# GLA in whole token groups, with new charges for two engines in the recorder of a hybrid decoder kernel

## Chip, cores and metric

The kernel runs on one core of one Trainium2 chip. The metric is device time in microseconds (us), the median of several runs. TensorE multiplies matrices; VectorE, ScalarE and GpSimd (DVE, ACT and POOL in the profile) do the rest; SyncE (SP) issues the DMAs.

## What is computed

A two-layer decoder trunk runs over 1072 tokens: 16 meta tokens and 8 sample sequences of 4 tokens (together 48 leading tokens) and a prompt of 1024. In each layer one input projection feeds four mixers with four heads each; their outputs are joined, projected, normalised, and followed by a SwiGLU feed-forward and a second normalisation.

```
for l in range(DEPTH):                      # 2
    proj = x @ w_in[l]                      # 1024 -> 3864
    o_a = gated DeltaNet(...)               # 4 heads, 64x64 state
    o_b = HGRN2(...)                        # 4 heads, 64x64 state
    o_c = GLA(c_q, c_k, c_v, log_sigmoid(c_lr @ gla_wg + gla_bg) / 16)   # 4 heads, 32x64 state
    o_d = RetNet(...)                       # 4 heads, 64x64 state
    x = layer_norm(ALPHA * x + concat(o_a, o_b, o_c, o_d) @ w_out[l])
    x = layer_norm(ALPHA * x + (silu(x @ w_g[l]) * (x @ w_u[l])) @ w_d[l])
```

HGRN2 and GLA share one recurrence: with b the running sum of the log gates, a chunk's scores are q_t k_s exp(b_t - b_s) for s <= t, its output is scores times v plus (q exp(b)) times the carried state, and the state goes on with exp(b_last).

## The kernel before

Tokens lie in three groups of 304, 384 and 384 columns (`GROUPS`). The first group holds the 48 leading tokens and two chunks of 128; the others hold three chunks each. Features lie on the 128 partitions.

**Main stream.** The dense products (`main`: `layer_in`, `layer_out`, `layer_ffn`) run through each weight tile for the three groups. Each product is three matmuls of split operands (high and low halves in float32r), all with the full 128x128 array, recorded by `mm` at L839. Weights come in by DMA and are split by ScalarE (L861) and VectorE (L870).

**Mixers.** They run while `layer_in` still projects for later mixers. Four workers, each with an arena of 3072 columns (`Arena`), take jobs (a mixer or half of its heads, and a token group) from a queue in the order delta, GLA, HGRN2, retention. `task_units` cuts a job into units: the leading tokens, then the whole chunks. `UNITS` takes all chunks of a group as one unit (two in the first group, three in the others); `HALVES` cuts the second and third group into a unit of two chunks and one of one chunk, and is used for GLA alone. A layer so has 24 units of the other mixers (six jobs with four units each) and six of GLA.

**One unit of GLA or HGRN2** (`gated`). A 128x128 score block is built in steps. The steps of `upper` (64, 32) fill the off-diagonal parts, those of `low` (for GLA s8, s2, s1; for HGRN2 s8 and b8) the 32x32 blocks on the diagonal. Each step subtracts gate sums, takes exponentials on ScalarE, multiplies by q and k, runs small products with tiles of 32 rows, and copies or selects the result out of PSUM. Then come k and v transposed (`rows`, L845 for the transposes), the state (`states_and_out`), the output, and the head norm (`norm_out`; `head_mean` there makes two matmuls with full tiles). GLA packs four heads of 32 features into 128 partitions, the others two heads of 64.

**Order.** Nothing is written in the order it runs. Each thread (main stream, workers, weights, norms) yields operations, and the recorder (`run`, `emit`) plays them on a clock of its own and each time appends the operation that could start first to its engine's program. An operation's charge (for example 68 + 1.042 n ns for VectorE with n columns) and `LATENCY` (from its end until another engine may use the result) make that clock; `SHARED` is added where VectorE and GpSimd work on SBUF side by side. A pair such as `copy2` or `tt2` goes to the engine that would end first. The engines then run their programs in order and wait on semaphores. Small tiles and full tiles don't mix on TensorE: `run` holds a change of tile mode back for a while (`HOLD`, `SLACK`), and `emit` charges `DRAIN` for it.

Of the kernel before, what the change touches and what calls it, by code (L numbers as in the profile page):

```python
# [334 lines left out]

LATENCY = {"PE": 196.0, "DVE": 138.0, "ACT": 158.0, "POOL": 92.0}
SHARED = 300.0

# [97 lines left out]
class Kern:  # L436
# [437 lines left out]
    def stt(self, out, a, s, b, op0, op1):  # L874
# [3 lines left out]
        if isinstance(s, V):  # L878
            rd.append(s)
            sc = s.ap  # L880
            ptr = 61
        return Op("DVE", 68 + ptr + 1.042 * out.n,
                  lambda: self.nc.vector.scalar_tensor_tensor(out=out.x(), in0=a.x(), scalar=sc, in1=b.x(), op0=op0, op1=op1),  # L883
# [8 lines left out]
    def ts(self, out, a, s1, op0, s2=None, op1=None, eng="DVE"):  # L892
# [14 lines left out]
        if eng == "DVE":  # L907
            return Op("DVE", 68 + ptr + rate * out.n, lambda: self.nc.vector.tensor_scalar(out=out.x(), in0=a.x(), **kw), rd, (out,))  # L908
        return Op("POOL", 245 + 0.83 * out.n, lambda: self.nc.gpsimd.tensor_scalar(out=out.x(), in0=a.x(), **kw), rd, (out,))

    def dcopy(self, out, a):
        rate = 1.042 if a.sp == "p" else 0.52
        return Op("DVE", 68 + rate * out.n, lambda: self.nc.vector.tensor_copy(out=out.x(), in_=a.x()), (a,), (out,))  # L913

# [3 lines left out]
    def pred(self, out, mask, data):  # L918
        return Op("DVE", 68 + 1.042 * out.n,
                  lambda: self.nc.vector.copy_predicated(out=out.x(), mask=mask, data=data.x()), (data, out), (out,))  # L920

    def scan(self, out, d0, d1):
        return Op("DVE", 68 + 1.042 * out.n,
                  lambda: self.nc.vector.tensor_tensor_scan(out=out.x(), data0=d0.x(), data1=d1.x(), initial=0.0, op0=MUL, op1=ADD),
                  (d0, d1), (out,))

    def t32(self, out, a):
        return Op("DVE", 68 + 1.042 * out.n, lambda: self.nc.vector.transpose(out=out.x(), in_=a.x()), (a,), (out,))

# [5 lines left out]
    def recip(self, out, a):  # L935
        return Op("DVE", 68 + 8.4 * out.n, lambda: self.nc.vector.reciprocal(out=out.x(), in_=a.x()), (a,), (out,))

    def red(self, out, a):
        return Op("DVE", 68 + 1.042 * a.n,
                  lambda: self.nc.vector.tensor_reduce(out=out.x(), in_=a.x(), axis=mybir.AxisListType.X, op=ADD), (a,), (out,))  # L940
# [72 lines left out]
    def ln_sums(self, srcs, m, st):  # L1013

        nc = self.nc
        for k, s in enumerate(srcs):
            o = st.ap[0:m, 6 * k:6 * k + 6]
            yield Op("DVE", 68 + 1.05 * 512, lambda o=o, s=s: nc.vector.bn_stats(out=o, in_=s.x()), (s,), (st,))  # L1018
        o, x = st.ap[0:m, 12:14], st.ap[0:m, 0:12]
# [517 lines left out]
    def gated(self, A, l, u, q, k, vs, b, es, K, first, low, upper, S, S0, bo_out, names, sf, spent):  # L1537
# [17 lines left out]
        a4 = None if lead else at.r("p (h a t) -> p h a t", h=H, t=128)  # L1555
        for m in list(first) if lead else list(upper) + list(low):
            wk = wq = None
# [27 lines left out]
            for j in range(H // 2):  # L1585
# [28 lines left out]
                if m == 64:  # L1614
                    yield self.copy2(a4[0:64, hs, :, 64:128], bp[0:64, :, 0:64 * nb].r("p h (a t) -> p h a t", a=nb))
                elif m == 32:
                    for z in range(2):
                        r = slice(64 * z, 64 * z + 32)
                        yield self.copy2(a4[r, hs, :, 64 * z + 32:64 * z + 64],
                                         bp[r, :, 0:32 * nb].r("p h (a t) -> p h a t", a=nb))  # L1620
# [22 lines left out]
        qe = A.alloc(n)  # L1643
        yield self.tt2(qe, q, eb, MUL)
        ke = A.alloc(n)
# [7 lines left out]
        yield self.act(AF.Exp, ke, ke, scale=es)  # L1653
        yield self.tt2(ke, ke, k, MUL)
        kt = A.alloc(nb * 128)
        A.free(b)
# [5 lines left out]
        self.free(*spent)  # L1662
        yield from self.states_and_out(A, l, u, qe, kt, vts, at, S, S0, eb, None, K, H, bo_out, names, sf)

# [64 lines left out]

    def states_and_out(self, A, l, u, qe, kt, vts, at, S, S0, eb, gam, K, H, bo_out, names, sf):  # L1730

# [15 lines left out]
        else:  # L1747
# [4 lines left out]
            for a in range(nb):  # L1752
                sc = gam[0] if gam else eb[:, 128 * a + 127:128 * a + 128]
                yield self.stt(S[a + 1], S[a], sc,
# [8 lines left out]
        for j in range(nv):  # L1763
# [10 lines left out]
            for k in range(2):  # L1774
                for a in range(nb):
                    for hh in range(2):
                        h = 2 * j + hh
                        o = bo[64 * hh:64 * hh + 64, bl * a:bl * a + bl]
                        x = h * nb + a
                        if k:  # L1780
                            r = slice(K * h, K * h + K)
                            yield self.mm(o, S[a][r], qe[r, 128 * a:128 * a + 128], False, a == nb - 1)
                        else:
                            yield self.mm(o, vv(h, a), at[:, 128 * x:128 * x + 128], a == 0, False)
            if j == nv - 1:
                A.free(qe, at, *vts)
            yield from bo_out(j, bo)
# [153 lines left out]
    def ret(self, A, l, hh, g, J):  # L1941
# [24 lines left out]
        for x in self.task_units(A, J, g, self.i["sr"][l, hh]):  # L1966
# [42 lines left out]
            if u[0] + n == gn:  # L2009
                self.free(*ins)  # L2010
            yield from self.states_and_out(A, l, u, qe, kt, [vt], at, S, S0, None, gam, 64, 2, done,
                                           (None, "rs%d%d" % (l, hh)), sf)
# [646 lines left out]
```

## Time and profile before

| | |
|---|---|
| median of 3 runs | 3121.15 us (3118.95 to 3122.83) |
| the profiled execution, its own time | 3118.43 us |
| its span, first to last instruction | 3116.3 us |
| busy: TensorE, VectorE, ScalarE, GpSimd | 2987.8, 1750.8, 1111.4, 391.2 us |
| mean granted TensorE clock | 0.986 of full |

The profile cuts the span into slices and gives each engine's busy share, lists groups of equal instructions with their mean duration and the idle time before them, and names for each wait who ended it. The first layer's mixers run from about 100 to 690 us, its feed-forward from about 800 to 1540; the second layer's mixers from 1560 to 2176 us, its feed-forward until about 3070. A matmul's row shows a longer duration than the distance to the next one, since matmuls overlap; distances are read from start times.

### The profile page before, as it was taken

How to read it: one execution, taken by the hardware profiler on the slowest of the kernel's cores; microseconds unless marked ns; L12 is line 12 of the kernel's file. 1: busy time of each engine (PE TensorE's matmuls, PEld its weight loads, DVE VectorE, ACT ScalarE, POOL GpSimd, SP SyncE). 2: the span in 40 equal slices, each digit the busy share in tenths (PEclk: the TensorE clock that was granted, in tenths of full speed). 3: DMA queues.
4: the chain of work that ended last, by engine and by line, in shares of the span. 5: the costliest groups of instructions: out<-in, count | busy, mean ns of one | idle time of the engine just before them, and what ended most of it. 6: DMA issues, size and time to landing. Idle time of an engine off the chain costs nothing.

```text
span 3116.3 us, 65676 instructions
## 1 busy us (share of the span) xinstructions
PE 2987.8 (96%) x27758; PEld 2712.0 (87%) x27758; DVE 1750.8 (56%) x4142; ACT 1111.4 (36%) x2313; POOL 391.2 (13%) x444
## 2 busy tenths in 40 slices
PE   7999999999999999999999999999899999999996
PEld 5788887888999999999977888888689999999996
DVE  8877668577533333333598676684674333333336
ACT  5445667443311111111263456664342111111113
POOL 3411111000600000000033111110014000000000
PEclk9999999999999999999999999999999999999998
DMA  6311121351211111111142111124311111111112
GB/s 208 107 50 34 60 65 53 105 183 37 75 48 41 41 48 49 47 48 41 46 137 86 36 55 62 59 65 139 122 55 55 46 50 48 48 42 47 48 41 76
DMA packets 120741, 210.54 MB, mean 68 GB/s; under 512 B 32304, under 2 KB 81200, under 8 KB 120320
## 3 DMA queue, kind: packets, MB, share of 16 engines
q1 hardware_dynamic: 120448, 206.36, 20.7%
q8 instruction: 217, 3.56, 0.5%
q14 instruction: 76, 0.62, 0.1%
HBM read 162.08 MB, written 39.84 MB: 65 GB/s over the span
## 4 chain that ended last, share of the span: by engine, by line
PE 66%; DVE 7%; ACT 2%; DMA 2%; issue 1%; POOL 1%; SPq 0%; DVEq 0%; ACTq 0%; POOLq 0%
PE banks L839 64%; DVE H L870 2%; PE banks L845 1%; DVE P L870 1%; DVE H L883 1%; DVE R L870 1%; ACT H L864 1%; ACT R L861 1%; DMA H<-OF 0%; DVE H L1018 0%; POOL R L872 0%; DVE H L908 0%; DMA P<-H 0%; ACT P L864 0%; DVE P L913 0%
## 5 line engine op out<-in xcount | busy, mean ns | idle before, releaser
L839 PE MATMUL banks<-R 128*128 128x384 f32 (+3 forms) x11840 | 2091.1, 332 | 28.3 <-DVE H L883 9.4
L839 PEld LDWEIGHTS banks<-R 128*128 128x128 f32 x11840 | 1926.0, 190 | 91.3 <-issue 14.1
L870 DVE TENSOR_TENSOR H<-H,banks 128x512 f32<-128x512 f32 (+5 forms) x708 | 401.1, 570 | 522.3 <-PE banks L839 518.0
L870 DVE TENSOR_TENSOR R<-H,R 128x1024 fp32r<-128x1024 f32 (+5 forms) x376 | 358.9, 967 | 444.7 <-ACT R L861 442.0
L861 ACT CAST R<-H 128x1024 fp32r<-128x1024 f32 (+4 forms) x361 | 285.9, 806 | 817.7 <-PE banks L839 720.8
L839 PE MATMUL banks<-R,P 128*128 128x512 f32 x1584 | 371.7, 394 | 0.0
L839 PEld LDWEIGHTS banks<-R,P 128*128 128x128 f32 x1584 | 296.2, 188 | 66.7 <-issue 0.5
L864 ACT ACTIVATE H<-H 128x384 f32<-128x384 f32 (+12 forms) x477 | 204.5, 445 | 206.2 <-DVE H L1020 86.0
L872 POOL TENSOR_TENSOR H<-H 128x256 f32<-128x256 f32 (+8 forms) x206 | 194.6, 962 | 290.6 <-ACT H L864 116.1
L839 PE MATMUL banks<-H 32*32 32x32 f32 (+11 forms) x5884 | 187.2, 224 | 18.8 <-DVE H L870 6.3
L872 POOL TENSOR_TENSOR P<-H,P 128x384 fp32r<-128x384 f32 (+1 forms) x22 | 39.5, 1798 | 1274.0 <-ACT P L861 1271.7
L839 PEld LDWEIGHTS banks<-H 32*32 32x32 f32 (+6 forms) x5884 | 133.3, 120 | 75.2 <-issue 39.3
L839 PE MATMUL banks<-P 32*32 32x32 f32 (+14 forms) x6240 | 181.1, 214 | 15.7 <-DVE P L870 9.8
L839 PEld LDWEIGHTS banks<-P 32*32 32x32 f32 (+10 forms) x6240 | 132.0, 117 | 63.4 <-issue 27.5
L861 ACT COPY H<-banks 128x384 f32<-128x384 f32 (+14 forms) x313 | 115.8, 376 | 181.2 <-PE banks L839 143.3
L870 DVE TENSOR_TENSOR H<-H 128x384 f32<-128x384 f32 (+14 forms) x389 | 155.3, 417 | 43.8 <-ACT H L864 25.7
L861 ACT CAST P<-H 128x304 fp32r<-128x304 f32 (+2 forms) x132 | 64.3, 487 | 284.5 <-DVE H L870 284.5
L864 ACT ACTIVATE H<-banks 128x384 f32<-128x384 f32 (+4 forms) x166 | 70.7, 430 | 222.5 <-PE banks L839 215.5
L839 PE MATMUL banks<-P,R 128*128 128x304 f32 (+1 forms) x1056 | 147.4, 299 | 0.0
L839 PEld LDWEIGHTS banks<-P,R 128*128 128x128 f32 x1056 | 145.9, 188 | 0.0
L845 PE MATMUL banks<-H 128*128 128x128 f32 (+4 forms) x642 | 109.0, 290 | 30.3 <-DMA H<-in_cst 7.7
L845 PEld LDWEIGHTS banks<-H 128*128 128x128 f32 (+4 forms) x642 | 74.7, 142 | 62.7 <-ACT H L864 17.3
(86 smaller groups left out, 1637.9 us busy)
## 6 DMA issues: line engine op xcount, KB each, us to landing
H<-in_wst SPq DMA_DIRECT2D x208, 512.0 KB, 3.3
XR<-H SPq DMA_DIRECT2D x12, 512.0 KB, 3.4
GF<-H SPq DMA_DIRECT2D x32, 192.0 KB, 1.9
H<-XR SPq DMA_DIRECT2D x4, 1536.0 KB, 7.0
H<-XR SPq DMA_DIRECT2D x42, 128.0 KB, 2.7
XR<-H SPq DMA_DIRECT2D x42, 128.0 KB, 2.0
H<-OF SPq DMA_DIRECT2D x27, 192.0 KB, 4.6
H<-in_xin SPq DMA_DIRECT2D x8, 512.0 KB, 8.2
```

The costliest lines, as they stand in the source:

```text
L839: return Op("PE", cost, lambda: self.nc.tensor.matmul(out=out.x(), lhsT=lhsT.ap, rhs=rhs.ap, start=start, stop=stop), (lhsT, rhs), (out,), ...
L845: return Op("PE", 0.83 * p + 2.5, lambda: self.nc.tensor.transpose(out=out.x(), in_=in_.ap, identity=i.ap), (in_,), (out,), 20, None, tile ...
L861: fn = lambda: self.nc.scalar.copy(out=out.x(), in_=in_.x())
L864: fn = lambda: self.nc.scalar.activation(out=out.x(), in_=in_.x(), func=f, scale=s, bias=b)
L870: lambda: self.nc.vector.tensor_tensor(out=out.x(), in0=a.x(), in1=b.x(), op=op), (a, b), (out,))
L872: lambda: self.nc.gpsimd.tensor_tensor(out=out.x(), in0=a.x(), in1=b.x(), op=op), (a, b), (out,), 27.0)
L883: lambda: self.nc.vector.scalar_tensor_tensor(out=out.x(), in0=a.x(), scalar=sc, in1=b.x(), op0=op0, op1=op1),
```

## The change

GLA takes all chunks of a group as one unit, as the other mixers do. To fit the arena, a unit now makes the low steps first and takes the full score blocks, one buffer for each pair of heads, only ahead of step 64; exp(b) is reused as q exp(b), with only its last columns copied to `eb`; the transposed v overwrites v where there are two v tiles. The charges of VectorE and ScalarE rise by 25 and by 52 to 54 ns an operation, `LATENCY` falls by 18 and 48 ns, `SHARED` rises by 50. `stt`, `ts`, `pred`, `scan`, `t32`, `recip`, `red` and `ln_sums` change like `tt` (68 becomes 93).

```diff
-LATENCY = {"PE": 196.0, "DVE": 138.0, "ACT": 158.0, "POOL": 92.0}
-SHARED = 300.0
+LATENCY = {"PE": 196.0, "DVE": 120.0, "ACT": 110.0, "POOL": 92.0}
+SHARED = 350.0
...
     def act(self, func, out, in_, scale=1.0, bias=0.0):
-        cost = out.n * 0.833 + (51 if in_.sp == "p" else 93)
+        cost = out.n * 0.833 + (105 if in_.sp == "p" else 145)
...
     def tt(self, out, a, b, op, eng="DVE"):
-            return Op("DVE", 68 + 1.042 * out.n,
+            return Op("DVE", 93 + 1.042 * out.n,
...
     def dcopy(self, out, a):
-        rate = 1.042 if a.sp == "p" else 0.52
-        return Op("DVE", 68 + rate * out.n, ...
+        rate = 1.042 if a.sp == "p" or len(out.ap.shape) > 2 else 0.52
+        return Op("DVE", 93 + rate * out.n, ...
...
     def gated(...):
-            at = A.alloc(nb * H * 128)
-            yield self.zero(at)
             ac = A.alloc(nb * H * 32)
             yield self.zero(ac)
-        for m in list(first) if lead else list(upper) + list(low):
+        for m in list(first) if lead else list(low) + list(upper):
+            if not lead and m == upper[0]:
+                at = [A.alloc(nb * 256) for _ in range(H // 2)]
+                for x in at:
+                    yield self.zero(x)
...
             for z in range(4):
-                yield self.dcopy(a4[r, :, :, 32 * z:32 * z + 32], dst[r].r("p h (a t) -> p h a t", t=32))
+                for j, x in enumerate(a4):
+                    yield self.dcopy(x[r, :, :, 32 * z:32 * z + 32],
+                                     dst[r, 2 * j:2 * j + 2].r("p h (a t) -> p h a t", t=32))
...
+            eb, qe = A.alloc(nb), eb
+            yield self.dcopy(eb, qe.r("p (a c) -> p a c", c=128)[:, :, 127])
+            yield self.tt2(qe, q, qe, MUL)
...
-        vts = [A.alloc(nb * 128) for _ in vs]
+        place = not lead and len(vs) > 1
+        vts = vs if place else [A.alloc(nb * 128) for _ in vs]
...
     def task_units(self, A, J, g, state):
-        units = (HALVES if J.key[1] == "c" else UNITS)[g]
+        units = UNITS[g]
```

What the recorder then writes differs on every engine. Counted over the whole programs, before and now: matmuls 21462 and 21446, VectorE instructions 4144 and 3948, ScalarE 2315 and 2174, GpSimd 449 and 462, SyncE 797 and 781. The TensorE program goes from full tiles to smaller ones or back 700 times before and 648 times now, that is, it has 350 and 324 runs of small-tile products.

**TensorE, first layer, the s8, s2 and s1 products of GLA** (rows `32x48`: 32 partitions, 48 columns; R is the region of split operands, so `banks<-R` rows are the main stream; H and P are the regions with the arenas; x counts equal rows). First, the program before at the one-chunk unit of the second token group: each step is a run of 16, and the same happens once more for the third group.

```order
L839 MATMUL banks<-H 32x48 x16
L839 MATMUL banks<-R 128x304 x10
L839 MATMUL banks<-R 128x384 x15
L839 MATMUL banks<-H 32x48 x16
L839 MATMUL banks<-R 128x48 x2
L839 MATMUL banks<-R 128x384 x9
L839 MATMUL banks<-H 32x48 x16
```

Then the changed program, where a step covers three chunks at once.

```order
L839 MATMUL banks<-P_74 32x512 x2
L839 MATMUL banks<-R 128x384 x18
L839 MATMUL banks<-H 32x48 x48
L839 MATMUL banks<-R 128x384 x20
L839 MATMUL banks<-R 128x304 x7
L839 MATMUL banks<-P_74 32x48 x32
L839 MATMUL banks<-R 128x304 x39
L839 MATMUL banks<-H 32x48 x48
```

The three runs of the one-chunk unit are gone, its products stand in the longer runs. The last `32x48` row of GLA in this layer comes after 1560 matmuls of the R region before and after 1125 now.

**TensorE, second layer, the end of the mixers**, where the output projection begins (`128x288` and `128x512` rows of R) and retention's last units are left. The program before:

```order
L839 MATMUL banks<-H 128x128 x6
L839 MATMUL banks<-P_14763 64x512 x2
L845 MATMUL banks<-H 128x128 x2
L839 MATMUL banks<-R 128x288 x15
L845 MATMUL banks<-H 128x128 x2
L839 MATMUL banks<-H 128x128 x4
L845 MATMUL banks<-H 128x128 x3
L839 MATMUL banks<-R 128x288 x4
L845 MATMUL banks<-H 128x128 x3
L839 MATMUL banks<-R 128x288 x5
L839 MATMUL banks<-R 128x512 x3
L839 MATMUL banks<-H 128x128 x6
```

The changed program:

```order
L839 MATMUL banks<-H 128x128 x6
L839 MATMUL banks<-P_14602 64x512 x2
L845 MATMUL banks<-H 128x128 x2
L839 MATMUL banks<-R 128x288 x24
L845 MATMUL banks<-H 128x128 x2
L839 MATMUL banks<-H 128x128 x4
L839 MATMUL banks<-P_14602 64x64 x4
L845 MATMUL banks<-H 128x128 x6
L839 MATMUL banks<-H 64x64 x6
L839 MATMUL banks<-P_14602 64x128 x4
L839 MATMUL banks<-P_14602,H 64x128 x2
L839 MATMUL banks<-P_14602 64x128 x2
```

The 24 products `128x288`, which stood in three pieces between the small ones, and the first `128x512` ones (3, 3 and 1) no longer separate them; the row of small products that begins behind the 24 goes on for 14 rows.

## Rows read from the trace of the kernel before

**Rows 1.** The page: span, and busy us of each engine.

```profile
span 3116.3 us, 65676 instructions
PE 2987.8 (96%) x27758; PEld 2712.0 (87%) x27758; DVE 1750.8 (56%) x4142; ACT 1111.4 (36%) x2313; POOL 391.2 (13%) x444
```

**Rows 2.** Stretches: from:to, length, busy PE, PEld, DVE, ACT, POOL, clock, DMA share, GB/s.

```profile
0.00:100.00 100.00, 77.97 (x515) 61.17 (x516) 89.79 (x251) 58.12 (x132) 35.76 (x47) 0.95 0.55 187
100.00:690.00 590.00, 560.28 (x8332) 484.75 (x8331) 412.05 (x1237) 316.92 (x729) 84.39 (x130) 0.98 0.26 81
690.00:800.00 110.00, 105.06 (x619) 90.39 (x618) 86.16 (x155) 47.34 (x88) 20.46 (x12) 0.98 0.18 55
800.00:1400.00 600.00, 600.00 (x3492) 575.08 (x3491) 217.39 (x315) 103.87 (x162) 47.09 (x33) 1.00 0.15 47
1560.00:2176.00 616.00, 586.48 (x8562) 512.43 (x8561) 447.72 (x1365) 336.48 (x785) 121.47 (x167) 0.98 0.25 77
2176.00:2340.00 164.00, 145.76 (x904) 121.52 (x903) 121.25 (x230) 66.56 (x132) 25.13 (x18) 0.96 0.30 97
2340.00:3000.00 660.00, 660.00 (x3887) 631.94 (x3886) 240.87 (x353) 116.15 (x182) 48.78 (x34) 1.00 0.14 47
3060.00:3117.00 57.00, 32.22 (x179) 28.55 (x177) 45.43 (x91) 19.80 (x33) 1.29 (x1) 0.81 0.21 76
```

**Rows 3.** Waits of TensorE, 100 to 690 us: total us, times, longest.

```profile
PE banks L839 <- DVE P L870: 8.7, 10, 1.4
PE banks L845 <- DVE P L870: 2.5, 3, 1.4
PE banks L839 <- DVE H L870: 2.4, 5, 1.1
```

**Rows 4.** Waits of TensorE, 1560 to 2176 us.

```profile
PE banks L839 <- DVE P L870: 9.9, 11, 3.0
PE banks L839 <- DVE H L870: 4.2, 6, 1.8
```

**Rows 5.** Timeline of TensorE, runs of small products: start, us, what, count.

```profile
89.07 0.31 PE L839 MATMUL banks<-P 32*32 32x32 f32 x8
89.31 1.42 PE L839 MATMUL banks<-R 128*128 128x304 f32 x8
...
215.08 0.62 PE L839 MATMUL banks<-P 32*32 32x32 f32 x48
215.63 1.39 PE L839 MATMUL banks<-R 128*128 128x304 f32 x8
...
226.57 0.91 PE L839 MATMUL banks<-P 32*32 32x32 f32 x80
227.41 0.82 PE L839 MATMUL banks<-R 128*128 128x304 f32 x4
```

**Rows 6.** Groups by shape, VectorE and ScalarE: busy us, mean ns, idle before.

```profile
L870 DVE TENSOR_TENSOR P<-P 128x256 f32<-128x256 f32 x44 | 18.7, 425 | 2.9 <-PE banks L839 2.3
L870 DVE TENSOR_TENSOR H<-H 128x128 f32<-128x128 f32 x58 | 17.3, 303 | 9.3 <-ACT H L864 7.2 <-PE banks L839 1.8
L870 DVE TENSOR_TENSOR P<-P 128x384 f32<-128x384 f32 x29 | 17.1, 588 | 0.3
```

**Rows 7.** Timeline, VectorE and ScalarE, equal instructions back to back.

```profile
3105.90 2.43 DVE L870 TENSOR_TENSOR H<-H 128x512 f32<-128x512 f32 x4
...
1613.44 1.34 ACT L864 ACTIVATE H<-H 128x384 f32<-128x384 f32 x3
```

**Rows 8.** Timeline of TensorE, second layer, end of the mixers; idle before in brackets.

```profile
2183.14 0.39 PE L839 MATMUL banks<-R 128*128 128x32 f32 x1 [4.18 <-ACT R L861]
...
2191.19 0.88 PE L845 MATMUL banks<-H 128*128 128x128 f32 x6 [2.15 <-DVE H L870]
...
2196.14 2.73 PE L839 MATMUL banks<-R 128*128 128x288 f32 x15 [1.84 <-DVE H L883]
```

**Rows 9.** Stretch around those waits (columns as in Rows 2).

```profile
2172.00:2202.00 30.00, 20.56 (x120) 17.64 (x119) 23.34 (x48) 16.99 (x38) 3.50 (x4) 0.83 0.81 269
```

More of the change, by code (lines that the diff above doesn't have):

```diff
@@ L881, in stt @@
             ptr = 61
-        return Op("DVE", 68 + ptr + 1.042 * out.n,
+        return Op("DVE", 93 + ptr + 1.042 * out.n,
                   lambda: self.nc.vector.scalar_tensor_tensor(out=out.x(), in0=a.x(), scalar=sc, in1=b.x(), op0=op0, op1=op1),
@@ L918, in pred @@
     def pred(self, out, mask, data):
-        return Op("DVE", 68 + 1.042 * out.n,
+        return Op("DVE", 93 + 1.042 * out.n,
                   lambda: self.nc.vector.copy_predicated(out=out.x(), mask=mask, data=data.x()), (data, out), (out,))
     def scan(self, out, d0, d1):
-        return Op("DVE", 68 + 1.042 * out.n,
+        return Op("DVE", 93 + 1.042 * out.n,
                   lambda: self.nc.vector.tensor_tensor_scan(out=out.x(), data0=d0.x(), data1=d1.x(), initial=0.0, op0=MUL, op1=ADD),
@@ L927, in t32 @@
     def t32(self, out, a):
-        return Op("DVE", 68 + 1.042 * out.n, lambda: self.nc.vector.transpose(out=out.x(), in_=a.x()), (a,), (out,))
+        return Op("DVE", 93 + 1.042 * out.n, lambda: self.nc.vector.transpose(out=out.x(), in_=a.x()), (a,), (out,))
     def zero(self, out, eng="POOL"):
@@ L935, in recip @@
     def recip(self, out, a):
-        return Op("DVE", 68 + 8.4 * out.n, lambda: self.nc.vector.reciprocal(out=out.x(), in_=a.x()), (a,), (out,))
+        return Op("DVE", 93 + 8.4 * out.n, lambda: self.nc.vector.reciprocal(out=out.x(), in_=a.x()), (a,), (out,))
     def red(self, out, a):
-        return Op("DVE", 68 + 1.042 * a.n,
+        return Op("DVE", 93 + 1.042 * a.n,
                   lambda: self.nc.vector.tensor_reduce(out=out.x(), in_=a.x(), axis=mybir.AxisListType.X, op=ADD), (a,), (out,))
@@ L1017, in ln_sums @@
             o = st.ap[0:m, 6 * k:6 * k + 6]
-            yield Op("DVE", 68 + 1.05 * 512, lambda o=o, s=s: nc.vector.bn_stats(out=o, in_=s.x()), (s,), (st,))
+            yield Op("DVE", 93 + 1.05 * 512, lambda o=o, s=s: nc.vector.bn_stats(out=o, in_=s.x()), (s,), (st,))
         o, x = st.ap[0:m, 12:14], st.ap[0:m, 0:12]
@@ L1554, in gated @@
             dst, mrows = ac.r("p (h x) -> p h x", h=H), 128
-        a4 = None if lead else at.r("p (h a t) -> p h a t", h=H, t=128)
-        for m in list(first) if lead else list(upper) + list(low):
+        for m in list(first) if lead else list(low) + list(upper):
[3 more added lines that the diff above has]
+                    yield self.zero(x)
+                a4 = [x.r("p (h a t) -> p h a t", h=2, t=128) for x in at]
             wk = wq = None
@@ L1642, in gated @@
         yield self.act(AF.Exp, eb, b, scale=es)
-        qe = A.alloc(n)
-        yield self.tt2(qe, q, eb, MUL)
+        if lead:
+            qe = A.alloc(n)
+            yield self.tt2(qe, q, eb, MUL)
+        else:
+            eb, qe = A.alloc(nb), eb
+            yield self.dcopy(eb, qe.r("p (a c) -> p a c", c=128)[:, :, 127])
+            yield self.tt2(qe, q, qe, MUL)
         ke = A.alloc(n)
@@ L1654, in gated @@
         yield self.tt2(ke, ke, k, MUL)
+        A.free(b)
         kt = A.alloc(nb * 128)
-        A.free(b)
         yield from self.rows(ke, nb, bl, [lambda x: iter([self.copy2(kt[0:bl], x[0:bl, 0:nb * 128])])])
         A.free(ke)
-        vts = [A.alloc(nb * 128) for _ in vs]
+        place = not lead and len(vs) > 1
+        vts = vs if place else [A.alloc(nb * 128) for _ in vs]
         for v, vt in zip(vs, vts):
             yield from self.rows(v, nb, bl, [lambda x: iter([self.copy2(vt[0:bl], x[0:bl, 0:nb * 128])])])
-        self.free(*spent)
-        yield from self.states_and_out(A, l, u, qe, kt, vts, at, S, S0, eb, None, K, H, bo_out, names, sf)
+        self.free(*(spent[:-len(vs)] if place else spent))
+        yield from self.states_and_out(A, l, u, qe, kt, vts, at, S, S0, eb, None, K, H, bo_out, names, sf, place, spent)
     def stepped(self, A, name, q, k, b, es, n):
@@ L1752, in states_and_out @@
             for a in range(nb):
-                sc = gam[0] if gam else eb[:, 128 * a + 127:128 * a + 128]
+                sc = gam[0] if gam else eb[:, a:a + 1]
                 yield self.stt(S[a + 1], S[a], sc,
@@ L1783, in states_and_out @@
                         else:
-                            yield self.mm(o, vv(h, a), at[:, 128 * x:128 * x + 128], a == 0, False)
+                            yield self.mm(o, vv(h, a), at[j][:, 128 * x:128 * x + 128], a == 0, False)
+            A.free(at[j])
             if j == nv - 1:
-                A.free(qe, at, *vts)
+                A.free(qe, *(() if place else vts))
+                if place:
+                    self.free(*spent[-len(vts):])
             yield from bo_out(j, bo)
@@ L2010, in ret @@
                 self.free(*ins)
-            yield from self.states_and_out(A, l, u, qe, kt, [vt], at, S, S0, None, gam, 64, 2, done,
+            yield from self.states_and_out(A, l, u, qe, kt, [vt], at if lead else [at], S, S0, None, gam, 64, 2, done,
                                            (None, "rs%d%d" % (l, hh)), sf)
```

12 lines of the change are left out of this document (6 added, 6 removed).

## Prediction

> **What bounds the kernel.** I read the page first. TensorE is busy 2987.8 of 3116.3 us, and no other engine more than 56% of the span [rows 1]. So the time is TensorE's work plus its gaps, 128.5 us, and an engine that is merely relieved gives nothing. Next I read the stretches, to see where the gaps are. In both feed-forwards TensorE is busy for all of 600 and all of 660 us: nothing to gain there, and the change touches nothing there but the order on engines that have time [rows 2]. The gaps lie in five places: 22.0 us in the first 100 us, 29.7 in the first layer's mixers (590 less 560.28), 29.5 in the second layer's (616 less 586.48), and 4.9 and 18.2 us around the output projection and the first norm of each layer [rows 2]; the rest, some 24, is nearly all at the very end, where the last norm has no matmuls left beside it [rows 2]. GLA runs only in the two mixer stretches, so its stake is their 59.2 us. Third, the waits in them: the longest total is VectorE's results in the arenas, 8.7 and 9.9 us in waits of about 0.9 us, followed by other waits on VectorE [rows 3, 4]. These are waits that the recorder did not foresee: it had main-stream matmuls at hand for most of the stretch and would have put some in between, had its clock shown the operand late.
>
> **TensorE's work.** 16 matmuls go, the head norm's two for each of the eight GLA outputs that were cut in two; the columns stay the same, so I take 0. Everything else TensorE computes is the same products in another order. What shrinks is the number of runs of small tiles: 350 to 324. The price of a run that doesn't depend on its length comes from start times: from the first small product to the next main one a run of 48 takes 0.55 us (215.08 to 215.63) and one of 80 takes 0.84 (226.57 to 227.41), so a product adds 0.29 / 32 = 0.009 us and 0.12 us is left; a run of 8 takes 0.24 (89.07 to 89.31), which leaves 0.17 [rows 5]. 26 runs at 0.15 are **-3.9 us**; the bounds are 0, if the saved runs only grow elsewhere, and -6.5, at 0.25 with a gap ahead of the run too.
>
> **VectorE and ScalarE.** A merged VectorE operation takes 588 ns instead of 425 + 303, so 140 ns less [rows 6]. 196 instructions fewer are about 27 us of its 1750.8, and 141 on ScalarE are of the same size. By themselves these give 0: TensorE covers them, being busy 95% of both stretches [rows 2]. The cover is gone only where TensorE already waits, which is the next term. Added inside a unit are four more copies of diagonal blocks (two buffers instead of one) and a copy of the last columns of exp(b). They stand in a chain of some 40 operations while other workers' products and the main stream keep TensorE going: 0, and within a unit well under what the second unit's removed chain saves. GpSimd's 13 more instructions fall on an engine with 13% load [rows 1]: 0. SyncE issues 16 DMAs less, the gate loads and output writes of the cut units; the DMA share is about 0.25 in these stretches [rows 2]: 0. The new order of low before upper puts two zero-fills later, which nobody waits for until step 64.
>
> **Waits in the mixers.** First, fewer units. Of 30 units a layer two go. If a unit's share of the gaps is even, 59.2 x 2/30 = **-3.9 us**. The bounds are 0 (the longer units wait more often) and -11.8 (all of the GLA units' even share, 6/30). That GLA's last step product moves from main matmul 1560 to 1125 in the first layer also frees a worker earlier, which I take as part of this term.
>
> Second, the charges. Charge plus latency of a 384-column VectorE operation goes from 468 + 138 = 606 to 493 + 120 = 613 ns, and for ScalarE from SBUF from 413 + 158 = 571 to 465 + 110 = 575: a single result is due as before. What changes is a queue: every operation behind another is now planned 25 or 52 ns later. The trace has both cases. Four 512-column VectorE operations back to back take 2.43 us; with the last one's own 0.67 or so taken off, three periods are 1.76, 0.59 each, where the old charge was 602 and the new one is 627 ns; on ScalarE three operations of 384 columns take 1.34, so a period of about 0.41, against 413 and 465 [rows 7]. Free-running queues are thus a little faster than planned now, and those broken by waits are slower. The recorder will place dependent products later than it did and fill with main matmuls, which is the safe side: waits should shrink. The bounds are -44, when all waits on VectorE in these stretches go, and +15, when the reshuffle opens as many new ones as a quarter of the 59.2. I take **-8**, a seventh of what is left, since the calibration of a single result hardly moves.
>
> The Trainium skill's page "VectorE: DVE Perf Modes", section "The TRN2 errata — SBUF-src ops pay a fixed extra latency per instruction", says that VectorE's latency is exposed between instructions and gives 691 ns for a float32 operation of 512 columns. By it the new charge would still be too small. The back-to-back row does not agree: it has 0.59 us for the period [rows 7]. Were the page right for these queues, the recorder would still plan too early and the term would be nearer to 0, which is the second rival below.
>
> **The sum.** 3118.43 (the profiled execution) - 3.9 - 3.9 - 8 = 3102.6. The median lies 2.7 above that execution, so I forecast **3105 us**, 16 less than before (0.5%). A measurement of this kernel can tell about 0.2%, 6.2 us, from no change.
>
> **Rivals.**
> - *The gaps close much further.* With GLA's work ahead of HGRN2's and retention's by some 400 main matmuls and a VectorE with 27 us less to do, the mixers could run ahead of the main stream, and then most waits on VectorE go (-35 of the 44), with both other terms: 3121 - 35 - 8 = **3078**. For it: the longest totals of waits are on VectorE [rows 3, 4]. Against: the units of the other mixers, 24 of 30, keep their chains.
> - *Nothing comes through.* The new charges miss the real queues as far as the old ones did, on the other side, and the greedy order shifts its waits elsewhere; only the runs are saved, or not even they: **3117 to 3122**. For it: each wait is about a microsecond, spread over dozens of places [rows 3, 4], and I find no single one that the change removes.
> - *Slower: the end of the second layer's mixers.* There the changed program has 24 main products in one piece and then 14 rows of retention's last units with no main product between. In the kernel before, the same place already waits 4.18, 2.15 and 1.84 us [rows 8], and its stretch loses 18.2 us [rows 2]. The 31 main products that no longer separate the rows are about 5 us of cover (24 at 0.13, 7 at 0.23), and if the bare rows then wait as long as the rows now do, 1.8 to 2.2 us for each of eight or ten more round trips, the stretch's gap doubles: +18. The granted clock falls too: it was 0.83 over the 30 us around these waits, so about a third of them, 10 us, ran at the lower level of 1.2 GHz and lost some 5 us [rows 9]; half of that again is +2.5. With the savings in the runs and units this gives 3121 + 20.5 - 8 = **3134**. It decides when the stretch loses over 34 us where it loses 18.2 now. The skill's page "TensorE: Matmul & The Clock Gate" ("HAM oscillation — how this bites in real kernels") has the same rule, that gaps between groups of matmuls make the next group start at the lower clock; the trace agrees [rows 9]. Against: retention's chain there is no longer than before, and the first layer's end has no such row.
>
> **Chances.** The forecast, 3088 to 3114, 0.46; the first rival, 3065 to 3088, 0.18; nothing, 3114 to 3126, 0.18; slower, 3126 to 3145, 0.18. The range leaves out the far ends: 3075 to 3132. Faster by over 0.2% (under 3114.9): 0.46 + 0.18 and the edge of the case of nothing, 0.65. Same: 0.17. Slower: 0.18.
>
> **What would show it.** Right: TensorE's busy time hardly changed, its gaps in the two mixer stretches down from 59.2 to about 45 us, VectorE some 25 us less busy, waits on VectorE's arena results shorter in total, the feed-forwards untouched. Wrong: gaps in the mixers as before (the charges did nothing), or a stretch at the second layer's output projection that loses over 30 us, or main-stream matmuls waiting for a PSUM bank or a weight, a wait that I leave out.

## The result, and the profile after

| | before | after |
|---|---|---|
| median, runs beside each other on one chip | 3120.05 us (4 runs) | 3085.26 us (4 runs) |
| lowest and highest | 3118.79 to 3122.83 | 3081.71 to 3093.02 |
| ratio | | 0.9891, 95% interval 0.9870 to 0.9911 |

The change makes the kernel 34.8 us faster (1.1%). The forecast was 16 us: the direction came, the time is inside the range, and the size is more than double.

The profiled execution of after is the longest of its four, 3093.02 us. The four stand in the order of their granted clock: 3093.02 us at 0.986, 3085.84 at 0.987, 3084.67 at 0.988, 3081.71 at 0.990. So some of the 34.8 us lies outside what this profile can show. Its page, span and engines, against [rows 1]:

```profile
span 3091.2 us, 65267 instructions
PE 2971.5 (96%) x27742; PEld 2709.6 (88%) x27742; DVE 1743.0 (56%) x3946; ACT 1080.6 (35%) x2172; POOL 405.6 (13%) x457
```

The span is 25.1 us shorter. Of that TensorE's busy time is 16.3 and its gaps are 8.8 (128.5 to 119.7). VectorE is only 7.8 us less busy, ScalarE 30.8 less, GpSimd 14.4 more. Part of this is that the recorder chose another engine for some of the copies and products that two can make: in e2 below, which has the charges alone, GpSimd has 30 instructions more (405.8 us), ScalarE 22 and VectorE 10 fewer. But the new charges aren't why VectorE gains so little: with the old ones, whole units leave it at 1742.4 (e1) and 1756.2 us (e10).

The stretches of [rows 2] at the mixers and at the end, in after (columns as there):

```profile
100.00:690.00 590.00, 563.44 (x8425) 494.73 (x8426) 422.17 (x1157) 311.24 (x672) 103.82 (x139) 0.99 0.27 83
1560.00:2176.00 616.00, 582.98 (x8638) 515.63 (x8637) 449.73 (x1290) 325.39 (x722) 119.96 (x170) 0.98 0.28 84
2176.00:2340.00 164.00, 151.36 (x841) 130.48 (x841) 113.10 (x192) 55.34 (x107) 40.37 (x27) 0.94 0.20 66
```

Read this way, the gaps of the two mixers are 26.6 and 33.0 us where they were 29.7 and 29.5: nothing seems to have come. But after is ahead by then, and equal times no longer hold equal work. A ruler is needed. The feed-forwards are one, since TensorE never waits in them, and the first transposes of the second layer are the mark at which the first one ends. They start here, in the timeline of TensorE before, and then after:

```profile
1535.30 1.91 PE L845 MATMUL banks<-H 128*48 128x128 f32 x16
```

```profile
1516.49 1.91 PE L845 MATMUL banks<-H 128*48 128x128 f32 x16
```

Stretches cut by that mark, of before and then of after (the first feed-forward is the third stretch):

```profile
100.00:800.00 700.00, 665.35 (x8949) 575.13 (x8948) 498.21 (x1390) 364.27 (x817) 104.85 (x142) 0.98 0.25 77
800.00:1535.30 735.30, 735.30 (x4283) 704.11 (x4282) 266.82 (x393) 125.14 (x194) 51.03 (x35) 1.00 0.14 46
1535.30:2340.00 804.70, 756.94 (x9601) 654.15 (x9600) 588.28 (x1633) 418.74 (x944) 147.58 (x186) 0.98 0.26 81
2340.00:3116.30 776.30, 752.22 (x4417) 717.41 (x4415) 307.68 (x478) 145.15 (x229) 51.98 (x36) 0.99 0.15 50
```

```profile
100.00:781.20 681.20, 653.11 (x8930) 572.17 (x8931) 491.84 (x1282) 349.95 (x746) 118.32 (x148) 0.99 0.25 78
781.20:1516.49 735.29, 735.29 (x4283) 704.10 (x4282) 267.94 (x395) 126.84 (x197) 53.13 (x36) 1.00 0.14 46
1516.49:2315.00 798.51, 752.82 (x9598) 655.92 (x9597) 585.99 (x1545) 402.92 (x869) 145.70 (x189) 0.97 0.26 82
2315.00:3091.20 776.20, 751.34 (x4412) 716.52 (x4410) 308.52 (x478) 144.91 (x229) 51.44 (x36) 0.99 0.15 50
```

The feed-forwards match to 0.1 us and nearly to the matmul, so the cuts are right. All of the 25 us lies in two places: the first layer's mixers and what follows them are 18.8 us shorter (12.2 of busy time, 6.6 of gaps), the second's 6.2 (4.1 and 2.1).

Where the busy time fell is told by the groups of TensorE by tile. The main stream's own products, before and then after:

```profile
L839 PE MATMUL banks<-R 128*128 128x384 f32 (+3 forms) x11840 | 2091.1, 332 | 28.3 <-DVE H L883 9.4 <-ACT R L861 4.6 <-DVE R L870 3.1
```

```profile
L839 PE MATMUL banks<-R 128*128 128x384 f32 (+2 forms) x11824 | 2075.5, 332 | 36.9 <-DVE H L883 16.4 <-DVE R L913 9.1 <-DVE R L870 9.1
```

They multiply the same columns in 15.6 us less. Of TensorE's 16.3 us in all, some 6 are the granted clock: in stretches of 8 us over the whole span, busy time times the missing share of the clock adds up to 29.5 us before and 23.2 after. (At the lower level of 1.2 GHz these `128x384` products start 320 ns apart, at the upper one 174.) Another 6 go with the 26 runs of small products that are gone. By the start times in both traces, the last full-tile product ahead of a run holds TensorE 0.10 us longer than its like inside a row, and the last small one ahead of a full tile 0.12 us longer; 0.22 us for each of 26 runs make 5.7. Some 4 us stay open. A busy TensorE therefore isn't a constant of the work. The Trainium skill's page "Trainium Kernel Development and Optimization", section "Performance Expectations", calls matmul busy time a bad measure of how close a kernel is to roofline, because matmuls are pipelined, and names the busy share of weight loads as one of two good ones. The trace is in keeping: PEld moved by 0.1% only, from 2712.0 to 2709.6, and PE by 0.5%.

Waits of TensorE in after, first 100 to 680 us, then 1540 to 2160 us, for [rows 3, 4]:

```profile
PE banks L839 <- DVE H L883: 6.0, 1, 6.0
PE banks L839 <- DVE R L870: 5.4, 8, 1.2
PE banks L839 <- DVE P L870: 2.5, 6, 0.6
```

```profile
PE banks L845 <- DVE H L870: 7.4, 2, 6.3
PE banks L839 <- DVE P L870: 5.6, 10, 1.4
PE banks L839 <- DVE H L883: 5.6, 5, 3.3
```

The many short waits on VectorE's products in the arenas (P, L870) fell from 8.7 to 2.5 and from 9.9 to 5.6 us. That is what was hoped for. In their place stand two long ones of about 6 us.

### The profile page after: what moved, and what is told of

It reads as the page before. It is cut to its first block, busy times and chain, and to the rows that moved or that the text cites. A ratio compares the mean times of both kernels' runs of the same rounds, so it can differ in the third digit from the quotient of the medians.

```text
span 3091.2 us, 65267 instructions
## 1 busy us (share of the span) xinstructions
PE 2971.5 (96%) x27742; PEld 2709.6 (88%) x27742; DVE 1743.0 (56%) x3946; ACT 1080.6 (35%) x2172; POOL 405.6 (13%) x457
## 4 chain that ended last, share of the span: by engine, by line
PE 71%; DVE 6%; ACT 2%; DMA 2%; issue 1%; POOL 1%; SPq 0%; DVEq 0%; ACTq 0%; POOLq 0%
PE banks L839 69%; PE banks L845 2%; DVE H L870 2%; DVE P L870 1%; DVE H L883 1%; DVE R L870 1%; ACT R L861 1%; DMA H<-in_wst 1%; ACT H L864 1%; DMA H<-OF 0%; ACT P L864 0%; DVE H L908 0%; DMA H<-XR 0%; ACT L651 0%; SPq L951 0%
## 5 line engine op out<-in xcount | busy, mean ns | idle before, releaser
L839 PE MATMUL banks<-R 128*128 128x384 f32 (+2 forms) x11824 | 2075.5, 332 | 36.9 <-DVE H L883 16.4
L839 PEld LDWEIGHTS banks<-R 128*128 128x128 f32 x11824 | 1922.9, 189 | 98.6 <-DVE R L870 15.8
L870 DVE TENSOR_TENSOR H<-H,banks 128x512 f32<-128x512 f32 (+5 forms) x714 | 403.7, 569 | 520.9 <-PE banks L839 517.7
L870 DVE TENSOR_TENSOR R<-H,R 128x1024 fp32r<-128x1024 f32 (+5 forms) x375 | 358.1, 971 | 454.4 <-ACT R L861 451.0
L861 ACT CAST R<-H 128x1024 fp32r<-128x1024 f32 (+3 forms) x353 | 281.1, 816 | 812.7 <-PE banks L839 719.2
L864 ACT ACTIVATE H<-H 128x384 f32<-128x384 f32 (+11 forms) x437 | 189.5, 452 | 175.1 <-DVE H L1020 74.7
L839 PE MATMUL banks<-H 32*32 32x32 f32 (+13 forms) x5724 | 191.3, 223 | 10.3 <-DVE H L883 2.7
L839 PE MATMUL banks<-P 32*32 32x32 f32 (+12 forms) x6240 | 170.0, 212 | 21.5 <-DVE P L870 9.5
L839 PEld LDWEIGHTS banks<-P 32*32 32x32 f32 (+8 forms) x6240 | 126.9, 116 | 65.2 <-issue 31.7
L861 ACT COPY H<-banks 128x384 f32<-128x384 f32 (+8 forms) x282 | 109.1, 391 | 191.4 <-PE banks L839 161.1
L870 DVE TENSOR_TENSOR H<-H 128x384 f32<-128x384 f32 (+14 forms) x310 | 137.2, 461 | 22.5 <-ACT H L864 16.6
L864 ACT ACTIVATE H<-banks 128x384 f32<-128x384 f32 (+5 forms) x166 | 70.6, 430 | 224.9 <-PE banks L839 216.4
L845 PE MATMUL banks<-H 128*128 128x128 f32 (+3 forms) x639 | 104.8, 285 | 24.7 <-DVE H L870 8.4
L845 PEld LDWEIGHTS banks<-H 128*128 128x128 f32 (+3 forms) x639 | 72.4, 140 | 53.8 <-DVE H L870 11.0
```

What stands on the lines that cost most here:

```text
L839: return Op("PE", cost, lambda: self.nc.tensor.matmul(out=out.x(), lhsT=lhsT.ap, rhs=rhs.ap, start=start, stop=stop), (lhsT, rhs), (out,), ...
L845: return Op("PE", 0.83 * p + 2.5, lambda: self.nc.tensor.transpose(out=out.x(), in_=in_.ap, identity=i.ap), (in_,), (out,), 20, None, tile ...
```

## The experiments

The questions were which part of the change brings the time, by what, and how much of it is the accident of one order. *Cut* means GLA in `HALVES`, *whole* GLA in `UNITS`. *Charges* are those per operation (with `SHARED` and the copy's rate), *latencies* those in `LATENCY`; old are those of before, new those of the change. All kernels here compute the whole of the reference. Times of before beside them were 3115.53 to 3118.93 us; only ratios to it are compared.

**Each part alone.** e1 is the change with the charges, `LATENCY` and `SHARED` of before; e2 is before with the new ones.

```diff
 e1 (after, all charges back)               e2 (before, all charges new)
-LATENCY = {... "DVE": 120.0, "ACT": 110.0  -LATENCY = {... "DVE": 138.0, "ACT": 158.0
+LATENCY = {... "DVE": 138.0, "ACT": 158.0  +LATENCY = {... "DVE": 120.0, "ACT": 110.0
...
-            return Op("DVE", 93 + ...      -            return Op("DVE", 68 + ...
+            return Op("DVE", 68 + ...      +            return Op("DVE", 93 + ...
```

> GLA in whole groups with the old charges. Forecast's theory (both parts add, -8 us each): 3112 us. All from GLA: 3083 to 3090. All from the charges: 3117 to 3123. Luck of the order: anywhere within 15 us of 3120, unrelated to the parts.

> The kernel before with the new charges, GLA still cut in two. Forecast's theory: 3112 us. All from GLA: 3117 to 3123. All from the charges: 3083 to 3090. If the parts add, the gains of this run and of GLA alone sum to 35 us.

Whole units alone: 3095.21 us, ratio 0.9925 (0.9909 to 0.9941), 23 us. Charges alone: 3102.24 us, 0.9949 (0.9933 to 0.9965), 16 us. Each part brings more than the sum of the prediction gave it, so by this pair of orders neither is idle and neither does it all.

**Cut units in the change, and a nudge.** e3 leaves everything new but cuts GLA. e4 is before with 4 ns more for TensorE's results: no reason to be better or worse, but another greedy order.

```diff
 e3 (after)
-        units = UNITS[g]
+        units = (HALVES if J.key[1] == "c" else UNITS)[g]
 e4 (before)
-LATENCY = {"PE": 196.0, ...
+LATENCY = {"PE": 200.0, ...
```

> The changed kernel with the cut units put back for GLA alone (new charges, new step order and buffers stay). Forecast's theory: some 8 us over the changed kernel, 3093. All from GLA's whole units: 3115 to 3123. All from the charges: 3083 to 3090. It also parts the whole units from the rest of the rewritten steps: without an effect of those it equals the charges alone.

> The kernel before with one charge nudged without a reason (latency of TensorE 196 to 200 ns), which reshuffles the order on every engine. If orders scatter little: 3117 to 3124. If the gain of the change is of the size of such scatter: more than 10 us from 3120 in either direction.

e3: 3114.19 us, 0.9993 (0.9981 to 1.0005). With cut units the change loses nearly everything. It differs from e2 only in the rewritten steps of a unit, and from it by 0.44%. e4: 3111.07 us, 0.9981 (0.9970 to 0.9992): a nudge without a reason is worth 6 us. So single orders have a scatter that one comparison can't see through, and the change had to be nudged too.

**The change nudged**, `LATENCY` of PE 196 to 200 (e5) and to 190 (e6).

> The changed kernel with TensorE's latency charge nudged from 196 to 200 ns, to see how far its own orders scatter. If the whole units and the charges are what gains: within 8 us of the changed kernel's 3085. If the changed kernel is one lucky order: 3100 or more.

> The same with 190 ns. Its program has 636 changes of tile mode against 648. Mechanism: 3078 to 3093. Lucky order: 3100 or more.

e5: 3075.51 us, 0.9876 (0.9857 to 0.9895). e6: 3092.34 us, 0.9926 (0.9912 to 0.9940). Three orders of the same change gain 34, 39 and 23 us, a mean of 32. The gain is real, its size is known to about 8 us. The pages of e5 and e6, span and engines:

```profile
span 3077.2 us, 65301 instructions
PE 2974.3 (97%) x27742; PEld 2712.7 (88%) x27742; DVE 1749.2 (57%) x3940; ACT 1087.2 (35%) x2186; POOL 392.1 (13%) x449
```

```profile
span 3091.1 us, 65291 instructions
PE 2975.7 (96%) x27742; PEld 2716.3 (88%) x27742; DVE 1740.0 (56%) x3947; ACT 1092.3 (35%) x2191; POOL 412.9 (13%) x445
```

So in the three orders TensorE's busy time is 16.3, 13.5 and 12.1 us lower than in before [rows 1], and its gaps are 8.8, 25.6 and 13.1 us shorter. By the sum over stretches of 8 us the clock is 6.3, 3.8 and 1.4 of the busy time; about 10 us are left in each. What differs from order to order is mostly the gaps.

**Is there a price for a unit or a run?** e7 cuts HGRN2 instead (eight units more in all), e8 cuts GLA in the second layer alone, e9 in the first alone.

```diff
 e7 (after)
-        units = UNITS[g]
+        units = (HALVES if J.key[1] == "b" else UNITS)[g]
 e8, e9 (after)
+        units = (HALVES if J.key[1] == "c" and J.key[0] == 1 else UNITS)[g]
+        units = (HALVES if J.key[1] == "c" and J.key[0] == 0 else UNITS)[g]
```

> The changed kernel with HGRN2 cut into units of two and one chunks instead, which adds eight units in the two layers where GLA's cut had four. If a unit has a price of its own (5 to 7 us each, as the two runs on GLA's cut say): 3125 to 3140. By the forecast's shares (some 2 us a unit for runs and gaps): 3095 to 3105. If only GLA's cut was harmful or the gain is the order's luck: 3080 to 3093.

> The changed kernel with GLA whole in the first layer alone, cut in the second. If each layer's whole units bring half of the 29 us between cut and whole under the new charges: about 3100. If all lies in one layer: near 3085 (the first) or 3114 (the second).

> The changed kernel with GLA cut in the first layer alone. The second layer's small products start at 1515 to 1517 us in all four programs so far that have whole units there and the new charges, at 1526 to 1528 with a cut (GLA's or HGRN2's). A price per unit: 1526 to 1529 here, and 3090 to 3100 in all. Luck: 1515 to 1520.

e7: 3091.27 us, 0.9920 (0.9903 to 0.9937), 9 us behind the change and within the scatter of its three orders. e8: 3097.24 us, 0.9936 (0.9919 to 0.9954). e9: 3088.54 us, 0.9908 (0.9891 to 0.9924). Whole units in one layer bring part of the gain whichever layer it is: against e3, 18 us in the first and 27 in the second, together more than the 32 of both. Eight more units of HGRN2 cost 9 us, four more of GLA between 11 (e11, below) and 32 (e3): a fixed price per unit isn't seen. The start of the second layer tells more than the whole time. It lies where the expectation of e9 had it for a price of cutting; e8, whole in the first layer, and then e9, cut there:

```profile
1514.97 1.91 PE L845 MATMUL banks<-H 128*48 128x128 f32 x16
```

```profile
1526.79 1.91 PE L845 MATMUL banks<-H 128*48 128x128 f32 x16
```

Under the charges and latencies of the change, by one profile each, the four programs with nothing cut in the first layer (after, e5, e6, e8) begin the second at 1515.0 to 1516.7 us, the five with a cut there (e2, e3, e7, e9, e11) at 1525.6 to 1528.2. So cutting costs about 11 us in the first layer, and as much for the four more units of HGRN2 there as for the two of GLA. In the second layer the orders scatter too much to tell.

**The parts alone, nudged; and the old latencies with the new charges.** e10 is e1 and e11 is e2, each with PE at 200. e12 is the change with `LATENCY` as before.

```diff
 e12 (after)
-LATENCY = {"PE": 196.0, "DVE": 120.0, "ACT": 110.0, "POOL": 92.0}
+LATENCY = {"PE": 196.0, "DVE": 138.0, "ACT": 158.0, "POOL": 92.0}
```

> Whole units with the old charges, TensorE's latency charge 200: a second order of this case. The whole units gain 20 us in either charges: 3092 to 3102, the second layer's start near 1525. If the first such order was lucky: 3108 or more.

> Cut units with the new charges, TensorE's latency charge 200: a second order of this case. The charges gain 6 to 15 us: 3100 to 3112, the second layer's start near 1527. If the charges give nothing of their own: 3115 to 3122.

> The changed kernel with the new charges but the old latencies (VectorE 138, ScalarE 158), so that single results too are planned 18 and 48 ns later. If planning later is what helps: 3075 to 3085. If the fit of a single result matters: 3092 to 3105. If neither: within its orders' scatter, 3077 to 3093.

e10: 3103.18 us, 0.9952 (0.9935 to 0.9968). e11: 3093.17 us, 0.9926 (0.9907 to 0.9945). e11 came out below the range expected for it. The parts change places, so which of them is larger can't be told; 15 to 23 us each. e12: 3069.65 us, 0.9844 (0.9826 to 0.9862), better than all three orders of the change and below every range expected. Unless this is one lucky order, the lower latencies of the change gave time back.

**Later still, and what is enough.** e13 is before with results due later by `LATENCY` alone. e14 is the change with latencies above the old ones. e15 is e12 nudged. e16 is e2 with the old latencies, so cut units, and e17 is e16 nudged. e18 is before with ScalarE's new charges alone.

```diff
 e13 (before)
+LATENCY = {"PE": 196.0, "DVE": 163.0, "ACT": 211.0, "POOL": 92.0}
 e14 (after)
+LATENCY = {"PE": 196.0, "DVE": 156.0, "ACT": 206.0, "POOL": 92.0}
 e15 (after), e17 (e2)
+LATENCY = {"PE": 200.0, "DVE": 138.0, "ACT": 158.0, "POOL": 92.0}
 e16 (e2)
+LATENCY = {"PE": 196.0, "DVE": 138.0, "ACT": 158.0, "POOL": 92.0}
 e18 (before)
-        cost = out.n * 0.833 + (51 if in_.sp == "p" else 93)
+        cost = out.n * 0.833 + (105 if in_.sp == "p" else 145)
```

> The kernel before with its old charges, but latencies raised by 25 (VectorE, 163) and 53 ns (ScalarE, 211), so that a single result is due about as in the kernel with new charges and old latencies, while queues run as planned before. If the due time of single results is what gains: 3100 to 3108. If it is the planned length of queues: 3112 to 3123.

> The changed kernel with latencies of 156 and 206, 36 and 96 ns over its own. If planning later always helps: 3062 to 3072. If there is a best margin near 18 and 48: 3075 to 3090. If the 3070 was one lucky order: 3080 to 3095.

> New charges, old latencies, whole units, TensorE's latency charge 200: a second order of the case that came out at 3070. If the later due time gains for itself: 3066 to 3078. If that order was lucky: 3080 to 3095.

> The kernel before with the new charges and the old latencies, GLA cut. With a price of cutting of 17 us as under the two other settings: 3083 to 3093. If the whole units bring little here: 3070 to 3080; if the later due time helps whole units alone: 3100 or more.

> Cut units, new charges, old latencies, TensorE's latency charge 200: a second order of the case that came out at 3070. If the charges alone bring what the whole change brings and more: 3066 to 3082. If that order was lucky and the whole units matter under every plan: 3085 or more.

> The kernel before with ScalarE's charges alone raised (51 to 105 and 93 to 145 ns), everything else old. If ScalarE's planned queue carries the gain of the charges: 3070 to 3090. If VectorE's does: 3112 to 3123. If they share it: 3090 to 3110.

e13: 3114.88 us, 0.9989 (0.9978 to 0.9999); e18: 3111.27 us, 0.9981 (0.9972 to 0.9989): neither does more than the nudge e4. e15: 3080.71 us, 0.9878 (0.9864 to 0.9891), which is in the range expected if the order of e12 was a lucky one. e16: 3069.57 us, 0.9847 (0.9834 to 0.9861), and e17: 3072.67 us, 0.9852 (0.9836 to 0.9869): with cut units and no new step, the charges (with `SHARED` and the copy's rate) alone bring 46 to 48 us as long as the latencies stay. e14: 3064.51 us, 0.9832 (0.9819 to 0.9845): the fastest of all, and faster than both kernels.

All by setting, gain over before in us (ratio times 3118):

| charges | latencies | GLA cut | GLA whole |
|---|---|---|---|
| old | old | 0, 6 (e4) | 23 (e1), 15 (e10) |
| old | raised | 3 (e13) | not run |
| new | lowered, as in the change | 16 (e2), 23 (e11), 2 (e3, new steps) | 34, 39 (e5), 23 (e6) |
| new | old | 48 (e16), 46 (e17) | 49 (e12), 38 (e15) |
| new | raised | not run | 52 (e14) |

The page of e16, span and engines, then its stretches cut at the mark of the second layer and at its last 776.2 us:

```profile
span 3070.5 us, 65694 instructions
PE 2969.1 (97%) x27758; PEld 2703.7 (88%) x27758; DVE 1767.4 (58%) x4127; ACT 1095.0 (36%) x2291; POOL 422.6 (14%) x481
```

```profile
0.00:1507.84 1507.84, 1468.64 (x13743) 1338.36 (x13744) 853.49 (x2016) 537.02 (x1132) 215.11 (x242) 0.99 0.22 70
1507.84:2294.30 786.46, 752.00 (x9629) 652.45 (x9628) 597.25 (x1635) 415.40 (x934) 163.15 (x207) 0.99 0.27 84
2294.30:3070.50 776.20, 748.42 (x4389) 712.94 (x4387) 316.65 (x477) 142.56 (x225) 44.33 (x33) 0.99 0.15 50
```

VectorE is 16.6 us busier than before [rows 1], and the kernel is 46 us shorter: the load on VectorE isn't what counts. Of the 45.8 us by which its span is shorter, 27.1 are gaps of TensorE; the clock's sum is 15.3 us instead of 29.5, so some 14 are the granted clock. The second layer's stretch is 12.0 us shorter than in after and 18.2 shorter than before, at 34.5 us of gaps against 45.7 and 47.8. The same stretches of e14:

```profile
0.00:1521.27 1521.27, 1466.90 (x13735) 1343.18 (x13736) 850.96 (x1918) 523.35 (x1068) 208.03 (x242) 0.99 0.22 70
1521.27:2287.50 766.23, 742.68 (x9598) 653.35 (x9597) 572.43 (x1519) 407.00 (x882) 149.32 (x199) 0.99 0.27 85
```

e14 is not better everywhere. Its first layer ends 13.4 us after that of e16, its second layer's stretch is 20.2 us shorter and loses only 23.6. Each plan meets the gaps of each layer anew; e14 may owe part of its lead to its order, since it wasn't nudged.

What follows: the new charges with the latencies kept are the larger lever, 46 us by themselves. What the whole units bring depends on the plan: 9 to 23 us under the old one (against both orders of it), 12 to 18 between the means under that of the change (without and with e3), and nothing that can be told in the whole time once charges are new and latencies old. There the profiles still have the second layer begin 9 us earlier with whole units (1499.2 and 1503.9 us in e12 and e15, 1507.8 and 1512.7 in e16 and e17), and take as much longer behind that. Under the change's own plan the parts add within the scatter (means of 19 and 20 alone, 32 together); with the latencies kept they don't. That they then take away the same waits is likely and not shown.

## Why the prediction was right or wrong

- **What bounds the kernel** held. The feed-forwards stayed as they were and all of the gain lies in the mixers and just behind them.
- **TensorE's work, taken at 0 but for the runs' 3.9: this is the step that failed.** "Busy time hardly changed" was to show the forecast right. It fell by 16.3, 13.5 and 12.1 us in the three orders of the change, at equal columns. The granted clock is 6.3, 3.8 and 1.4 of that; the sum of the prediction has no term for it, though its rival of a slower end does. About 10 us stay in each order, where 3.9 were foreseen.
- **The runs, -3.9 us,** were mis-sized: their price was read on the way out of a run alone, 0.12 to 0.17 us. The way in costs 0.10 more, so 26 runs are worth about 6 us, which is inside the stated bounds. It isn't what ranks the kernels: changes of tile mode were 700 before, 648 in the change, and 692 and 710 in e16 and e17, which are among the fastest.
- **VectorE and ScalarE at 0 by themselves** held, and e16 shows it best. That VectorE would be some 25 us less busy didn't come: 7.8, and no more with the old charges; why isn't settled.
- **Fewer units, -3.9 us, and the charges, -8: the two terms of "Waits in the mixers" were too small, each for itself.** Alone in two orders each, whole units brought 23 and 15 us, runs and units together foreseen at 7.8; the charges 16 and 23. In gaps of TensorE that is 13.6 and 9.8 us for the whole units, 10.3 and 17.0 for the charges. Their sum of 11.9 is not far from the change's gaps (8.8, 25.6 and 13.1, a mean of 15.8), but in part by luck: each was too small, and together they bring less than the two alone. The short waits on VectorE shrank, as the stated mechanism has it; that dependent products planned later and main products in between did this is argued and not shown. The reason given for the small value failed: "a seventh of what is left, since the calibration of a single result hardly moves". That the due time of a single result stays was correct and beside the point. e13 and e16 plan a single result for the same moment, 25 and 53 ns later than before; only e16 also lets the queue be occupied for so long, and it alone has the new `SHARED` and copy's rate. The first brings 3 us, no more than a nudge, the second 48. That the bound of -44 is near to this is chance: it counted waits, and e16's gaps fell by 27.1. The change took part of the gain back with its latencies: 32 and 23 us by cut units (e2 against e16, e11 against e17), about 11 by whole ones (mean of e12 and e15 against that of three orders), which is within their scatter.
- **Which charge it is** isn't settled. ScalarE's alone bring 6 us (e18), no more than a nudge, so VectorE's, `SHARED`, the copy's rate or both engines' together should do it. These weren't tried apart, so it isn't shown either that the time in the queue is what matters. The charges also move work between engines (GpSimd has 481 instructions in e16, 444 in before), but that doesn't rank the kernels: e2, with 474, gains 16 us, and e15, with 451, gains 38.
- **The rule on VectorE's charge.** By the Trainium skill's page "VectorE: DVE Perf Modes", section "The TRN2 errata — SBUF-src ops pay a fixed extra latency per instruction", the new charge was still too small: its 691 ns are the duration of one operation, and 512-column products of L870 last nearly as long here, 678 ns on average in before. The back-to-back row has 0.59 us between starts [rows 7]. So the new charge, 627 ns, is not too small for a free queue, and yet e12, e16 and e14 gain by planning later than the change does. The best plan isn't the one that is true of a free queue. Why not, no run shows; it may be that an operation which waits for another engine holds up its queue, and that a main product put in too early costs little.
- **The gaps close much further (3078)** was the nearest rival, and by its own road only in part: the short waits went, long ones came. e12 and e16 reach its time with another plan, but not by its price, nearly all waits on VectorE gone: their gaps are 25.3 and 27.1 us shorter, and 18.1 and 18.7 us are busy time.
- **Slower, at the end of the second layer's mixers**, didn't come: the whole stretch from the mark loses 45.7 us instead of 47.8. TensorE there in after, for [rows 8]:

```profile
2154.64 1.54 PE L845 MATMUL banks<-H 128*128 128x128 f32 x6 [6.25 <-DVE H L870]
...
2159.93 4.96 PE L839 MATMUL banks<-R 128*128 128x288 f32 x24
2164.73 0.38 PE L845 MATMUL banks<-H 128*128 128x128 f32 x2
2165.04 0.72 PE L839 MATMUL banks<-H 64*128 64x128 f32 x8
...
2166.07 1.10 PE L845 MATMUL banks<-H 128*128 128x128 f32 x6
...
2170.17 1.63 PE L839 MATMUL banks<-H 128*64 128x128 f32 x24
...
2175.39 1.36 PE L839 MATMUL banks<-R 128*128 128x256 f32 x3 [1.36 <-DVE R L913]
...
2198.17 2.07 PE L839 MATMUL banks<-R 128*128 128x512 f32 x4 [6.29 <-DVE H L883]
```

The 14 bare rows behind the 24 products run without one wait, where 1.8 to 2.2 us each were feared: their operands were ready, probably since VectorE had caught up in the 6.25 us before. Rows that the order lists side by side need not depend on each other. The clock part of that rival is there: 0.66 of full between 2140 and 2165 us, 0.66 again between 2190 and 2205, but 1.00 in the bare rows themselves:

```profile
2140.00:2165.00 25.00, 16.49 (x81) 13.94 (x81) 19.95 (x44) 11.66 (x28) 0.60 (x1) 0.66 0.63 202
2165.00:2176.00 11.00, 9.37 (x127) 6.98 (x126) 5.96 (x17) 3.34 (x8) 0.00 (x0) 1.00 0.21 51
...
2190.00:2205.00 15.00, 8.71 (x33) 6.42 (x33) 5.35 (x9) 0.65 (x2) 1.24 (x1) 0.66 0.32 118
```

So around the long waits TensorE runs partly at the lower level of 1.2 GHz, and in a row of small products without waits it doesn't.

## What to carry to other kernels

In this greedy plan, charging the operations of VectorE and ScalarE more brought 46 us, and planning single results as late by the latency alone brought 3; so try the charges on the late side, and don't take them back from the latency. Judge a change of a planner over several nudged orders, as differences of a third of a per cent come from nothing. Look at the busy time of the engine that bounds the kernel and not only at its gaps: here it fell by 12 to 16 us at equal work. Two parts of a change may add under one plan and not under another: measure each alone and in the other's presence.

## What was not expected of the hardware

Four nanoseconds in the plan, nothing else, move the time by 2 us (e17) to 11 (e15) on 3100, six by 11 (e6): the order of the same work alone is worth that. And TensorE's busy time for equal products ranges from 2992.6 us in e4 to 2969.1 in e16, a spread of 0.8%, while the load of its weights in these two differs by 0.4% (2714.7 and 2703.7). The granted clock alone doesn't rank the kernels: e14, the fastest, has 0.986 in its profile, as before has. Between the executions of one kernel it counts for much, as the four of after show.
